# Background operations of ScalarE and VectorE ordered behind the newest weight split of their engine, and the gate logarithms' exponential taken ahead of the copies

## The chip, the core and the metric

The kernel runs on one core of one Trainium2 chip. The metric is the device time of one execution in microseconds (us). The core has five engines with instruction queues of their own: TensorE (PE, matrix products), ScalarE (ACT, element functions and copies), VectorE (DVE, two-operand arithmetic), GpSimd (POOL) and SyncE (SP, which here only issues DMAs). Each engine works through its queue in the order of the program; engines wait for each other by semaphores. PE reads its operands from the on-chip memory (SBUF) and adds into accumulators (PSUM).

## The reference

A trunk of two layers over 256 positions of width 2048. Each layer normalises its input, multiplies it by one wide matrix `w_in`, runs eight mLSTM heads (matrix memory, part A) and eight RG-LRU blocks (gated linear recurrence, part B) side by side, multiplies both results by `w_out` and adds them to the input. A last normalisation follows. Everything is float32.

```python
def hybrid_layer(x, ...):
    u = rms_norm(x, norm_g)
    qk, v, o, z_a, ig, fg, xb, z_b = jnp.split(u @ w_in, SPLIT_AT, axis=-1)
    q, k = jnp.split(jax.nn.silu(causal_dwconv(qk, qk_conv)), 2, axis=-1)
    i_pre = ig + i_bias
    log_f = jax.nn.log_sigmoid(fg + f_bias)
    h = mlstm_chunkwise(q, k * DK_A ** -0.5, v, i_pre, log_f)
    h = h * jax.nn.sigmoid(o)
    h = ((h - mu) * lax.rsqrt(var + EPS)) * head_norm_g      # per head
    y_a = h * jax.nn.silu(z_a)
    xc = causal_dwconv(xb, lru_conv_w) + lru_conv_b
    y_b = rg_lru(xc, w_a, b_a, w_x, b_x, lam) * jax.nn.silu(z_b)
    return x + jnp.concatenate([y_a, y_b], axis=-1) @ w_out

def rg_lru(x, w_a, b_a, w_x, b_x, lam):
    r, i = sigmoid(x @ w_a + b_a), sigmoid(x @ w_x + b_x)    # in blocks of 256
    a = jnp.exp(-8.0 * r * softplus(-lam))
    u = x * i * jnp.sqrt(1 - a * a)
    return scan(h_t = a_t * h_{t-1} + u_t)
```

The mLSTM's result at time t needs exponentials of differences of the gates' running sums: `exp(F_t - F_s + i_s - m_t)` for s up to t. The kernel takes all 256 positions as one chunk.

## The kernel before

**Products.** A float32 product is made of three products in a shorter float format: each operand is split into a high part H and a rest L, and H·H, H·L and L·H are added. The weights come from DRAM in 268 tiles of 128 x 2048 (`raw`), each of them two halves, called units here and numbered 1 to 536 in the order of the program. `prepare` splits a unit: ScalarE copies it rounded (`wH`, line 308), VectorE subtracts (`wL`, `tt_`, lines 167–168). Twelve matmuls on PE (`mm_a`, line 332) use the unit; the second of them is the first that needs `wL`. The pool `wsp` holds four units' H and L, so `wH` of unit k must wait until PE is done with unit k-4, and the splits run at most three units ahead of PE.

**Everything else** (normalisation, convolutions, gates, recurrences, the heads' small products, the layout changes through DRAM that `swapped` makes) runs on ScalarE, VectorE and GpSimd between the splits. These background operations are written as Python generators in the list `bg`. After each unit's matmuls the main loop (lines 1099–1114) calls `pump`, which lets the generators issue operations until a budget of estimated us is spent; a generator that yields "wait" is passed over. The order in which `pump` issues is only the order of writing: a scheduler of the framework then fixes the order of each engine's queue, and places an operation whose inputs are ready earlier ahead of splits that were written before it. `order(a, b)` adds a dependence without a semaphore: a stands behind b in the queue, nothing else.

**The places that matter below.** For each layer l there are four head groups g of two heads.

- `rms_stats`, `rms_bcast`: the layer's normalisation factor `rstd` (sum, square root with a table load on ScalarE, reciprocal on VectorE); it is laid along the diagonal in `dg`, which PE multiplies with ones (`ps_rb`) and VectorE copies to `rb`. `o_post` uses `rstd` in the sigmoid `so`, which empties the accumulator of the layer's first chunk.
- `gates_gen`, `gates_tr`: the heads' input and forget gates as 8 rows; their running sums leave for DRAM (`nG_d`, line 538), their transposed values `sb` are copied by GpSimd into 128 rows (`at`, line 554, eight copies), and one half of the copies is exponentiated (`em`, line 555).
- `e_gen`: `nb` (line 564, GpSimd's DMA queue) reads `nG_d` back on all rows; VectorE adds, ScalarE exponentiates `E` (line 576), GpSimd clears the upper triangle (`affine_select`, line 579). There is one `nb` and one `E`.
- `qk_post`, `xb_post`, `zb_post`: a chunk of `u @ w_in` is scaled by ScalarE (`tok`), transposed by VectorE, moved by four SP DMAs (`moved`) and fetched back by a DMA of GpSimd's queue (`fr`, line 450). ScalarE then copies it (`ch`, line 470), and the convolution (`qc`, `xc`) follows.
- `gate_half`, `gate_post`: the RG-LRU gates. Sigmoids, exponentials and tanh on ScalarE, then on VectorE `gate1·xc`, `Dt`, `a`, `Dt`, `a`, `gate1·Dt`, `gate1·gate0` and four scans `xc` (line 795); `zb_post` makes `zb`, `ybH` and `ybL` of them, `z_post` makes `yaH` and `yaL`; these four are PE's operands in the products with `w_out`.

ScalarE's functions live in tables; where the next function isn't in the loaded table, an ACT_TABLE_LOAD stands ahead of it.

## Time and profile before

| | |
|---|---|
| time, median of 3 runs | 1495.64 us (1495.3 to 1496.07) |
| the profiled execution's own time | 1495.12 us |
| its span in the trace | 1493.4 us |
| mean granted TensorE clock | 0.999 |
| VectorE / ScalarE / GpSimd busy | 1049.7 / 915.3 / 75.5 us |
| DMA | 345.66 MB, 231 GB/s mean |

The span is what the trace covers from the first to the last instruction; the execution's own time is 1.7 us longer, for what lies around it. A row of a timeline reads: start, duration, engine, line, operation, out<-in, shape, and in brackets how long the engine had been idle before and what ended it; "x2" joins two instructions of a kind that follow each other. Matmuls overlap: each is drawn 0.39 us long, while the next starts 0.23 us after it.

### The profile page before, as it was taken

What the parts mean: (1) busy time and instruction counts of PE and PEld (TensorE: products, weight loads), DVE (VectorE), ACT (ScalarE), POOL (GpSimd) and SP (SyncE); (2) the same over time, 40 slices, a digit from 0 to 9 for tenths busy, and PEclk for the clock granted to TensorE, in tenths of its full rate; (3) what the DMA queues carried; (4) which work ended last, traced back from release to release, by engine and by line L of the source; (5) the groups of instructions that cost most, each with busy time, mean ns of one, the idle gap of its engine ahead of it and who ended that gap; (6) DMA issues with size and microseconds to landing.
All of it is one profiled execution on the core that took longest, in us unless ns stands there. A gap on an engine that the chain in (4) does not pass through costs nothing.

```text
span 1493.4 us, 18544 instructions
## 1 busy us (share of the span) xinstructions
PE 1482.0 (99%) x6894; PEld 1240.3 (83%) x6894; DVE 1049.7 (70%) x1406; ACT 915.3 (61%) x1160; POOL 75.5 (5%) x154
## 2 busy tenths in 40 slices
PE   9999999999999999999999999999999999999997
PEld 7888888888888888888888888888888888888886
DVE  6778976675567855678867697766855778556785
ACT  6656754575456854558675577645754567555675
POOL 0010000000000000000000200000000000000002
PEclk9999999999999999999999999999999999999999
DMA  9866667866577666876786667568666776578783
GB/s 329 303 224 220 222 224 210 253 225 215 200 239 233 216 224 218 259 255 226 264 287 195 227 211 247 196 210 251 222 227 210 226 239 227 205 229 265 232 282 112
DMA packets 91370, 345.66 MB, mean 231 GB/s; under 512 B 9984, under 2 KB 30480, under 8 KB 69776
## 3 DMA queue, kind: packets, MB, share of 16 engines
q1 hardware_dynamic: 79472, 306.44, 60.2%
q0 software_dynamic: 9344, 33.58, 9.1%
q10 hardware_dynamic: 2464, 4.47, 0.8%
q8 instruction: 54, 0.88, 0.2%
q14 instruction: 36, 0.29, 0.1%
HBM read 307.20 MB, written 37.24 MB: 231 GB/s over the span
## 4 chain that ended last, share of the span: by engine, by line
PE 94%; DVE 2%; ACT 1%; DMA 1%; issue 1%; POOL 0%; SPq 0%; ACTq 0%; DVEq 0%; POOLq 0%
PE acc L332 84%; PE ps_gt L751 3%; PE acc L345 1%; DVE wL L168 1%; PE acc L993 1%; PE acc L992 1%; PE acc L994 1%; DMA fr<-moved 1%; PE acc_x L993 0%; PE acc_x L992 0%; PE acc_x L994 0%; DMA raw<-in_ws_dram 0%; ACT wH L308 0%; PE ps_n L587 0%; PE ps_n L585 0%
## 5 line engine op out<-in xcount | busy, mean ns | idle before, releaser
L332 PE MATMUL acc<-wH,x_s 128*128 128x512 f32 x3008 | 930.4, 389 | 0.9 <-ACT wH L308 0.9
L168 DVE TENSOR_TENSOR wL<-raw,wH 128x1024 fp32r<-128x1024 f32 (+1 forms) x532 | 636.2, 1203 | 352.0 <-ACT wH L308 351.8
L308 ACT CAST wH<-raw 128x1024 fp32r<-128x1024 f32 (+1 forms) x532 | 547.0, 1037 | 393.2 <-PE acc L332 353.6
L332 PEld LDWEIGHTS acc<-wH,x_s 128*128 128x128 f32 x3008 | 564.5, 188 | 118.6 <-ACT wH L308 1.8
L332 PE MATMUL acc<-wL,x_s 128*128 128x512 f32 x1504 | 584.2, 389 | 0.9 <-DVE wL L168 0.8
L332 PEld LDWEIGHTS acc<-wL,x_s 128*128 128x128 f32 x1504 | 282.3, 188 | 59.6 <-DVE wL L168 1.6
L332 PE MATMUL acc<-wH,yaH 128*128 128x512 f32 x224 | 87.4, 390 | 0.0
L332 PE MATMUL acc<-wH,ybL 128*128 128x512 f32 x224 | 87.3, 390 | 0.0
L332 PE MATMUL acc<-wH,yaL 128*128 128x512 f32 x224 | 87.2, 389 | 0.0
L332 PE MATMUL acc<-wL,ybH 128*128 128x512 f32 x224 | 87.2, 389 | 0.0
L332 PE MATMUL acc<-wH,ybH 128*128 128x512 f32 x224 | 87.2, 389 | 0.0
L332 PE MATMUL acc<-wL,yaH 128*128 128x512 f32 x224 | 87.2, 389 | 0.0
L450 POOL DMA_DIRECT2D fr<-moved x34 | 18.8, 552 | 729.3 <-DMA moved<-blk 561.6
L332 PEld LDWEIGHTS acc<-wH,ybL 128*128 128x128 f32 x224 | 42.0, 188 | 9.0 <-DVE ybL L168 0.3
L332 PEld LDWEIGHTS acc<-wH,yaL 128*128 128x128 f32 x224 | 42.1, 188 | 9.0
L332 PEld LDWEIGHTS acc<-wH,ybH 128*128 128x128 f32 x224 | 42.1, 188 | 8.5
L332 PEld LDWEIGHTS acc<-wL,ybH 128*128 128x128 f32 x224 | 42.1, 188 | 8.5
L332 PEld LDWEIGHTS acc<-wL,yaH 128*128 128x128 f32 x224 | 42.1, 188 | 8.3
L332 PEld LDWEIGHTS acc<-wH,yaH 128*128 128x128 f32 x224 | 42.1, 188 | 8.2
L446 DVE STREAM_TRANSPOSE blk<-tok 128x1024 f32<-128x1024 f32 x33 | 40.8, 1237 | 11.0 <-ACT tok L436 11.0
L436 ACT ACTIVATE tok<-acc,rstd 128x512 f32<-128x512 f32 x46 | 29.1, 685 | 31.1 <-PE acc L332 31.0
L890 ACT COPY stage<-acc 128x1024 f32<-128x1024 f32 x24 | 24.4, 1015 | 34.4 <-PE acc L332 34.2
(209 smaller groups left out, 1291.9 us busy)
## 6 DMA issues: line engine op xcount, KB each, us to landing
raw<-in_ws_dram SPq DMA_DIRECT2D x168, 1024.0 KB, 5.2
raw<-in_ws_dram SPq DMA_DIRECT2D x190, 512.0 KB, 5.1
fr<-moved POOLq DMA_DIRECT2D x34, 512.0 KB, 6.9
moved<-blk SPq DMA_DIRECT2D x132, 128.0 KB, 2.6
x_d<-stage POOLq DMA_DIRECT2D x24, 512.0 KB, 5.5
x_d<-x_acc ACTq DMA_DIRECT2D x8, 512.0 KB, 8.4
x_acc<-x_d SPq DMA_DIRECT2D x8, 512.0 KB, 4.2
xp<-in_xt_dram SPq DMA_DIRECT2D x8, 256.0 KB, 7.2
```

The lines of the kernel that those rows point to most:

```text
L168: return V.tensor_tensor(out=o, in0=a, in1=b, op=op)
L308: st["wH"] = S.copy(out=H[:, o], in_=r[:, o])
L332: st["mm"] = PE.matmul(o, a_[:, kt, P * t : P * t + P], W[:, k], start=b, stop=z)
L345: PE.matmul(ps[:, ct, T * part : 2 * T], W[:, k, P * ct : P * ct + P], moving, start=first and k == 0 and part == 0, stop=last and k == 3 ...
L436: S.activation(out=by_block(tok, t), in_=acc[:, t, :].rearrange("p (c m j) -> p c m j", c=4, m=4), func=AF.Copy, scale=rstd[:, t : t + 1])
L446: V.transpose(out=blk.rearrange("p m n -> p (m n)"), in_=tok.rearrange("p m c t j -> p (m c t j)"))
L450: back.dma_start(out=fr.rearrange("p a c t i -> p a (c t i)"), in_=moved)
L751: PE.matmul(o, W[:, ib, jl], xs[:, ib, a, :], start=j == 0 and i == 0 and W is Hv and a == 0, stop=i == 1 and W is Lv, skip_group_check=True)
L890: S.copy(out=stage, in_=ps)
L992: PE.matmul(o, yH[:, kt, tsl], Hv[:, k, cs], start=start and k == 0, stop=False)
L993: PE.matmul(o, yH[:, kt, tsl], Lv[:, k, cs], start=False, stop=False)
L994: PE.matmul(o, yL[:, kt, tsl], Hv[:, k, cs], start=False, stop=stop and k == 1)
```

## The change

The change has three parts. First, the handles of VectorE and ScalarE are wrapped (`Behind`): while `pump` runs, from the ninth unit on (`st["tie"]`), every operation that it issues on VectorE is ordered behind the newest `wL`, and every one on ScalarE behind the newest `wH`. As `prepare` has run three units ahead by then, the newest split belongs to the unit three later than the one whose matmuls have just been issued; the scheduler can no longer put the operation ahead of that split. Second, in `gates_tr` the fixed number of waits is replaced by one for the first `nb`; the exponential is taken on `sb[32:64]` in place (32 x 256) ahead of GpSimd's copies, and the copies are ordered behind the `nb` DMA. Third, the exponential of `E` and the square root of `sd` are ordered behind the newest `wH`.

```diff
+    class Behind:
+        def __init__(self, eng, key):
+            self.eng, self.key = eng, key
+        def __getattr__(self, name):
+            op = getattr(self.eng, name)
+            if name == "dma_start":
+                return op
+            def f(*a, **k):
+                ins = op(*a, **k)
+                if st.get("tie"):
+                    order(ins, st[self.key])
+                return ins
+            return f
+    V, S = Behind(V, "wL"), Behind(S, "wH")
...
     def gates_tr(l):
         yield None
         yield None
-        for _ in range(2 + 2 * l):
+        while ("nb", l, 0) not in st:
             yield "wait"
+        sb = st["sb"]
+        order(S.activation(out=sb[32:64], in_=sb[32:64], func=AF.Exp), st["wH"])
...
-                G.tensor_copy(out=at[q_][32 * a : 32 * a + 32], in_=sv[32 * q_ : 32 * q_ + 32, :, a, 0:NH])
-        S.activation(out=em, in_=em, func=AF.Exp)
+                cp = G.tensor_copy(out=at[q_][32 * a : 32 * a + 32], in_=sv[32 * q_ : 32 * q_ + 32, :, a, 0:NH])
+                order(cp, st["nb", l, 0])
...
-        nc.gpsimd.dma_start(out=nb.rearrange("p h t -> p (h t)"), in_=src)
+        st["nb", l, g] = nc.gpsimd.dma_start(out=nb.rearrange("p h t -> p (h t)"), in_=src)
...
-        S.activation(out=E, in_=E, func=AF.Exp)
+        order(S.activation(out=E, in_=E, func=AF.Exp), st["wH"])
...
-            S.activation(out=sd, in_=mv[:, :, :, 1], func=AF.Sqrt, bias=epst)
+            order(S.activation(out=sd, in_=mv[:, :, :, 1], func=AF.Sqrt, bias=epst), st["wH"])
...
+        st["tie"] = n >= 8
         pump(1.05 if len(bg) <= 2 else 2.6)
+        st["tie"] = False
```

In the changed program nearly every operation of ScalarE and VectorE bears the wrapper's line, 101; and ScalarE has 62 table loads where it had 56. The rest of the instructions are the same, in other places; PE's order is the same but for four rows at the boundary of the layers.

**VectorE, first layer, first group, units 62 to 67** (the RG-LRU gates, with `yaL` of part A; gate_1450 is `gate1`, gate_1415 is `gate0`; "x2" stands for two of a kind). Before:

```order
175 L171 SCALAR_TENSOR_TENSOR a<-gate_1415,Dt 128x1024
176 L168 TENSOR_TENSOR wL<-raw,wH 128x1024 x2
177 L171 SCALAR_TENSOR_TENSOR Dt<-a,Dt 128x1024
178 L176 TENSOR_SCALAR a<-Dt 128x1024
179 L171 SCALAR_TENSOR_TENSOR gate_1450<-gate_1450,Dt 128x1024
180 L168 TENSOR_TENSOR wL<-raw,wH 128x1024
181 L168 TENSOR_TENSOR gate_1450<-gate_1450,gate_1415 128x1024
182 L168 TENSOR_TENSOR wL<-raw,wH 128x1024
183 L795 SCALAR_TENSOR_TENSOR xc<-a,gate_1450 128x256 x3
184 L168 TENSOR_TENSOR wL<-raw,wH 128x1024
185 L795 SCALAR_TENSOR_TENSOR xc<-a,gate_1450 128x256
186 L168 TENSOR_TENSOR wL<-raw,wH 128x1024
```

and with the change:

```order
171 L101 TENSOR_TENSOR wL<-raw,wH 128x1024
172 L101 SCALAR_TENSOR_TENSOR a<-gate_1415,Dt 128x1024
173 L101 TENSOR_TENSOR wL<-raw,wH 128x1024
174 L101 SCALAR_TENSOR_TENSOR Dt<-a,Dt 128x1024
175 L101 TENSOR_TENSOR wL<-raw,wH 128x1024
176 L101 TENSOR_SCALAR a<-Dt 128x1024
177 L101 SCALAR_TENSOR_TENSOR gate_1450<-gate_1450,Dt 128x1024
178 L101 TENSOR_TENSOR wL<-raw,wH 128x1024
179 L101 TENSOR_TENSOR gate_1450<-gate_1450,gate_1415 128x1024
180 L101 TENSOR_TENSOR yaL<-tok,yaH 128x1024
181 L101 SCALAR_TENSOR_TENSOR xc<-a,gate_1450 128x256 x4
182 L101 TENSOR_TENSOR wL<-raw,wH 128x1024
```

Row 176 of before holds the `wL` of units 62 and 63; row 171 of the change is that of unit 63, row 186 and row 182 are that of unit 67. Three gate operations (`gate1·xc`, the first `Dt`, and `a`) stood ahead of unit 62's split; now the first two stand between the splits of units 62 and 63, and `a` behind that of 63. `gate1·gate0` and the scans lay between three splits, and `yaL` behind unit 67's; now `gate1·gate0`, `yaL` and all four scans stand together ahead of unit 67's. The second layer has the same rows, at units 326 to 331.

**ScalarE, start of the second layer, units 288 to 292** (`rstd` and `so`; `gwp` are the gates' weights). Before:

```order
363 L383 ACT_TABLE_LOAD
364 L383 ACTIVATE rstd<-ms,epst 128x2
365 L308 CAST wH<-raw 128x1024 x2
366 L463 ACTIVATE tok<-fr,pars 128x256 x4
367 L308 CAST wH<-raw 128x1024
368 L465 CAST x_s<-tok 128x4x256
369 L308 CAST wH<-raw 128x1024 x6
370 L596 ACT_TABLE_LOAD
371 L596 ACTIVATE so<-acc,rstd 128x512 x2
372 L308 CAST wH<-raw 128x1024 x2
373 L436 ACTIVATE tok<-acc,rstd 128x4x4x32 x2
```

and with the change:

```order
384 L101 CAST x_s<-tok 128x4x256
385 L101 CAST wH<-raw 128x1024 x6
386 L101 CAST gwp<-gwr_105 128x8x8 x4
387 L101 CAST wH<-raw 128x1024
388 L101 ACT_TABLE_LOAD
389 L101 ACTIVATE rstd<-ms,epst 128x2
390 L101 CAST wH<-raw 128x1024
391 L101 ACT_TABLE_LOAD
392 L101 ACTIVATE so<-acc,rstd 128x512 x2
393 L101 ACTIVATE tok<-acc,rstd 128x4x4x32 x2
```

The square root of `rstd` with its table load stood nine splits ahead of `so`; now only one split, unit 291's, lies between them, and a second table load.

**GpSimd, first layer, second group** (the fetch `fr` of the q and k chunk is row 28 in both). Before:

```order
24 L564 DMA nb<-nG_d_117 128x512
25 L579 AFFINE_SELECT E<-E 128x128 x4
26 L450 DMA fr<-moved 128x1024
27 L604 MEMSET vH 128x4x2
28 L450 DMA fr<-moved 128x1024
```

and with the change:

```order
24 L470 DMA fr<-moved 128x1024 x2
25 L626 MEMSET vH 128x4x2
26 L586 DMA nb<-nG_d_117 128x512
27 L601 AFFINE_SELECT E<-E 128x128 x4
28 L470 DMA fr<-moved 128x1024
```

The group's `affine_select`, which waits for the exponential of `E` on ScalarE, and the next `nb`, which waits for VectorE's reads of the old one, have moved from well ahead of that `fr` to directly ahead of it. On ScalarE the exponential of this `E` now stands behind the split of unit 73, and the copy `ch` that waits for the `fr` behind that of unit 75, as before.

## The prediction

> **What bounds the kernel now.** I read the busy shares first, then the chain that ended last, then what PE waits for.

> ```profile
> PE 1482.0 (99%) x6894; PEld 1240.3 (83%) x6894; DVE 1049.7 (70%) x1406; ACT 915.3 (61%) x1160; POOL 75.5 (5%) x154
> PE 94%; DVE 2%; ACT 1%; DMA 1%; issue 1%; POOL 0%; SPq 0%; ACTq 0%; DVEq 0%; POOLq 0%
> L308 ACT CAST wH<-raw 128x1024 fp32r<-128x1024 f32 (+1 forms) x532 | 547.0, 1037 | 393.2 <-PE acc L332 353.6
> ```

> PE is busy 99% of the span, and the chain is PE for 94%. The third row says who waits for whom: ScalarE stood idle 353.6 us ahead of `wH` until PE released a buffer. The splits are ready early, so an operation on ScalarE or VectorE costs nothing until it makes a split late. The question is only where PE stands still, before and after.

> ```profile
> PE acc L332 <- ACT wH L308: 0.9, 1, 0.9
> PE acc L332 <- DVE wL L168: 0.8, 1, 0.8
> 839.40 0.74 PE L332 MATMUL acc<-wH,x_s 128*128 128x512 f32 x2
> 840.94 0.50 PE L332 MATMUL acc<-wL,x_s 128*128 128x512 f32 x1 [0.80 <-DVE wL L168]
> 898.81 0.61 PE L332 MATMUL acc<-wH,x_s 128*128 128x512 f32 x2
> 899.48 0.50 PE L332 MATMUL acc<-wL,x_s 128*128 128x512 f32 x1
> ```

> In the waits of PE just two stand against the splits. The second is that at 840.94: after two matmuls from 839.40, one each 0.23, it was due at 839.87 and came 1.07 late. A smaller one hides at 899.48, due at 899.27: 0.21. A matmul behind a stall is drawn 0.50 instead of 0.39, and its follower comes 0.11 later still. So the two stalls together hold 1.07 + 0.21 + 0.22 = **1.5 us**. That is all that the change can take out: 0.1%.

> **The part on the gates takes it out.**

> ```profile
> 828.17 4.72 POOL L554 COPY at<-scs 32x16 f32<-32x16 f32 x8
> 832.84 0.56 POOL L564 DMA_DIRECT2D nb<-nG_d  x1
> 832.92 0.21 ACT L555 ACTIVATE at<-at 128x16 f32<-128x16 f32 x1 [5.64 <-POOL at L554]
> ```

> ScalarE stood 5.64 us for GpSimd's eight copies, with splits queued behind; that made unit 306 late at 840.94. With the exponential ahead of the copies this goes. `nb` may now leave about 4.7 us earlier and the copies follow, so VectorE's use of both comes at much the same time; behind it `wL` of units 304 to 309 stay tight. Between nothing and a second stall of about half the old one I take **+0.3** (0 to 0.6). The stall at 899.48 goes because `a` no longer stands ahead of unit 326's split. Credit **-1.5**.

> **The RG-LRU gates behind the splits, twice.** In before these VectorE operations filled the wait for unit 326's `wH`; tied, they cannot.

> ```profile
> 157.10 1.04 ACT L308 CAST wH<-raw 128x1024 fp32r<-128x1024 f32 x1
> 896.94 1.99 ACT L308 CAST wH<-raw 128x1024 fp32r<-128x1024 f32 x2
> 895.46 0.69 DVE L176 TENSOR_SCALAR Dt<-Dt 128x1024 f32<-128x1024 f32 x1 [1.00 <-ACT Dt L768]
> 897.06 1.23 DVE L171 SCALAR_TENSOR_TENSOR a<-gate,Dt 128x1024 f32<-128x1024 f32 x1 [0.91 <-ACT gate L774]
> 898.21 2.35 DVE L168 TENSOR_TENSOR wL<-raw,wH 128x1024 fp32r<-128x1024 f32 x2
> ...
> 910.36 1.20 DVE L168 TENSOR_TENSOR wL<-raw,wH 128x1024 fp32r<-128x1024 f32 x1
> 911.48 1.22 DVE L168 TENSOR_TENSOR yaL<-tok,yaH 128x1024 fp32r<-128x1024 f32 x1
> 173.54 0.39 PE L332 MATMUL acc<-wL,x_s 128*128 128x512 f32 x1
> 913.22 0.39 PE L332 MATMUL acc<-wL,x_s 128*128 128x512 f32 x1
> ```

> Rows by engine: the `wH` of units 62 and 326, VectorE from 895.46, and the matmuls that need `wL` of units 67 and 331. From the start of unit 326's `wL` (898.21) to that of unit 331's (910.36) VectorE ran without a gap for 12.15. The new order puts four more operations into that stretch: `gate1·xc` and `yaL`, 1.14 each (1.22 less an overlap of 0.08 with what follows), `a`, 1.15 (897.06 to 898.21), and `Dt`, 0.61 (0.69 less the overlap). That is 16.2; with the split's 1.20, 17.4; less about 0.1 for a dependent pair that is no longer adjacent, 17.3. The stretch can start when `wH` is done: at 157.10 + 1.04 + 0.05 = 158.19 in the first layer, 898.03 in the second. So unit 67's `wL` ends at 175.5, and its matmul stood at 173.54: **+1.9**. Unit 331's ends at 915.3; its matmul, 0.32 earlier without the old stall, at 912.9: **+2.4**. Nothing else hides this: the cover was VectorE's idle time ahead of units 62 and 326. After the stall the splits of units 68 to 70 have 0.2 to 0.5 us left by the same count.

> **GpSimd's queue, twice.** `fr` of the second group now stands behind `nb` and `affine_select`, hence behind ScalarE's exponential of `E`.

> ```profile
> 183.19 0.53 POOL L450 DMA_DIRECT2D fr<-moved  x1 [12.32 <-ACT wH L308]
> L579 POOL TENSOR_SCALAR_AFFINE_SELECT E<-E x32: 282/284/659, 88.9 to 1193.6; 128x128 f32<-128x128 f32 x32
> L576 ACT ACTIVATE E<-E x8: 846/847/852, 87.9 to 1191.9; 128x768 f32<-128x768 f32 x8
> 181.68 1.06 ACT L308 CAST wH<-raw 128x1024 fp32r<-128x1024 f32 x1 [1.61 <-PE acc L332]
> 192.12 1.05 ACT L470 COPY ch<-fr 128x1024 f32<-128x1024 f32 x1 [3.94 <-DMA fr<-moved]
> 195.29 2.44 DVE L171 SCALAR_TENSOR_TENSOR qc<-ch,pars,qc 128x255 f32<-128x255 f32 x6
> 198.02 0.39 PE L332 MATMUL acc<-wL,x_s 128*128 128x512 f32 x1
> 200.74 0.39 PE L332 MATMUL acc<-wL,x_s 128*128 128x512 f32 x1
> ```

> All times here keep step with PE. The split of unit 73 ends at 182.74; a table load (1.28), `E` (0.85) and four selections (0.66 and three of 0.28) follow: about 186.4, so `fr` is issued 3.2 us later than at 183.19. If it again takes 8.9 us, `ch` starts near 195.4 and `wH` of unit 76 stands behind it: done at 197.5, its `wL` at 198.7, needed at 198.02: 0.7 to 0.9. Six convolution operations (2.44) lie ahead of unit 77's `wL`: 202.4, needed at 200.74 plus what is lost already: another 0.9. So at most 1.8; nothing if `fr` lands in its median of 6.9 us (the table of DMA issues). I take **+1.2**. The second layer has the same rows with `fr` at 922.81 landing in 8.4: at most 0.9, **+0.5**. In the third and fourth groups the splits behind `ch` are over 4 us early: nothing.

> **The start of the second layer.**

> ```profile
> 781.34 1.05 ACT L308 CAST wH<-raw 128x1024 fp32r<-128x1024 f32 x1 [1.67 <-PE acc L332]
> 782.41 1.28 ACT L596 ACT_TABLE_LOAD   x1
> 784.06 1.27 ACT L596 ACTIVATE so<-acc,rstd 128x512 f32<-128x512 f32 x2 [0.37 <-PE acc L332]
> 789.07 0.62 PE L332 MATMUL acc<-wH,x_s 128*128 128x512 f32 x2
> ```

> `so` empties the accumulator that unit 289's first matmul takes at 789.30 (the second of the last row). Now `rstd` is behind unit 290's `wH`, which PE releases one unit (2.72) after 781.34: 784.06 to 785.11; table and square root to 786.7; unit 291's `wH`, released at 786.78, to 787.83; table to 789.1; `so` to 790.4. **+1.1**.

> **Two smaller places.**

> ```profile
> 47.47 0.48 DVE L175 TENSOR_SCALAR dg<-ident,rstd 128x128 fp32r<-128x128 f32 x2
> 48.40 1.22 DVE L168 TENSOR_TENSOR wL<-raw,wH 128x1024 fp32r<-128x1024 f32 x1
> 49.60 0.40 PE L400 MATMUL ps_rb<-dg,ones 128*128 128x256 f32 x2
> 713.47 0.69 DVE L168 TENSOR_TENSOR zb<-zsg,xc 128x512 f32<-128x512 f32 x1
> 714.28 1.22 DVE L168 TENSOR_TENSOR wL<-raw,wH 128x1024 fp32r<-128x1024 f32 x1
> 715.66 0.39 PE L332 MATMUL acc<-wH,ybH 128*128 128x512 f32 x1
> ```

> At 47.47 four `dg` operations (0.93 to 48.40) trade places with unit 24's split. They end at about 50.4, and the second `ps_rb` matmul stood at 49.7: **+0.6**. At the boundary `zb` (0.69) comes behind unit 264's split (to 715.5) and `ybH` behind that, about 716.8, needed at 715.66: 1.1 late, unless PE's four moved rows cover it. Between 0 and 1.1 I take **+0.5**.

> **Sum.** -1.5 + 0.3 + 1.9 + 2.4 + 1.2 + 0.5 + 1.1 + 0.6 + 0.5 = 7.0, and 0.11 for each of some five restarts: **+7.5 us**. From the profiled execution's own 1495.12 that gives **1502.6**; the median, 1495.64, is 0.5 above that execution, which is inside the runs' spread. With every open cost at its lower end the sum is 4.9 (1500.0), at its upper end 9.5 (1504.6).

> The six added table loads (6 x 1.28 = 7.7 us) cost nothing by themselves, ScalarE being 61% busy, except in the chains above, where they are counted. [...] The trace bears out the load alone: at 782.41 the load begins 0.02 after the split and the engine is free at 783.69.

> **The rivals.**

> - *The bursts don't reach PE* (15%). The place is `wH` of units 62 and 326: if ScalarE reaches them 1.9 and 2.4 us sooner, VectorE's stretch starts sooner and both stalls vanish, and with them 4.3 + 0.2. For it: by PE alone these `wH` could run earlier; they stand behind exponentials and tanh. Against it: those eight operations and their table load keep their place. With the open costs at their lower ends this gives 1495.12 + 4.9 - 4.5 = 1495.5, not slower.
> - *Only the sure terms at about half* (13%): the bursts alone, all else covered: 1495.12 - 1.5 + 4.3 + 0.2 = 1498.1, at the border of what can be told.
> - *Only the credit* (3%): every tie hidden: 1493.6.
> - *More than counted* (14%). GpSimd's queue is strict, so every group's `fr`, not only the second's, may come late, or ScalarE's blocks pass on from one split to the next. Where a delay spreads over one more unit it costs its size again, 0.9 to 1.8 at four places: about 1507. [...]
> - *The forecast*, 1499 to 1505: 55%.

> A measurement of this kernel can tell about 0.2% (3 us) from no change. The range of 1496.5 to 1506.5 leaves out the rival of the credit, half of the first and a part of the fourth. Faster by over 0.2%, below 1492.6, needs more than all stalls that there are: 1%, out of the third rival. Within 0.2%: the rest of the first three rivals, 30%. Slower: the forecast and the fourth rival, 69%.

> **What would show it.** In the profile after: PE waiting for `wL` near 173 and 915, about 2 us each; for `so` near 790; near 198 behind `ch`; no wait near 840 and none of ScalarE for `at`. I am wrong if VectorE is idle ahead of units 67 and 331, or if `fr` of the second group is issued less than 2 us later against PE than before.

## The result, and the profile after

| | before | changed |
|---|---|---|
| time, median | 1495.64 us (1494.96 to 1496.07, 5 runs) | 1504.77 us (1502.46 to 1506.11, 5 runs) |
| ratio, 95% interval | 1 | 1.0062 (1.0052 to 1.0073) |
| profiled execution's own time / span | 1495.12 / 1493.4 us | 1505.44 / 1503.7 us |

The change costs 9.1 us, 0.6%. The forecast was 1502.6, in a range of 1496.5 to 1506.5.

From the page of the changed kernel, the busy line and the group of `wH`:

```profile
PE 1486.5 (99%) x6894; PEld 1241.5 (83%) x6894; DVE 1062.6 (71%) x1406; ACT 924.2 (61%) x1166; POOL 72.8 (5%) x154
L101 ACT CAST wH<-raw 128x1024 fp32r<-128x1024 f32 (+1 forms) x532 | 547.9, 1037 | 410.0 <-PE acc L352 369.0
```

Nothing stands out here: the engines do the same work, and ScalarE waits for PE even longer than before. (The page's chain, PE 94% before, reads PE 44% here only because it could be followed back no further than the wait for `so` at 797.) The loss is in places, and the waits of PE in the changed kernel show them (sum, times, longest):

```profile
PE acc L352 <- DVE wL L101: 5.6, 6, 1.8
PE ps_blank L130 <- DVE blank L101: 1.3, 1, 1.3
PE acc L352 <- ACT so L101: 1.0, 1, 1.0
PE acc L352 <- ACT ybH L101: 0.3, 1, 0.3
PE ps_rb L420 <- DVE dg L101: 0.3, 1, 0.3
PE acc L352 <- ACT wH L101: 0.2, 1, 0.2
```

Here a wait counts only from the drawn end of the last matmul, so each place loses more than its row says. Counted from start to start over PE's matmuls, with what follows at once (a matmul behind a stall starts 0.11 later than it should), the places are:

| near (us) | what came late | forecast | lost |
|---|---|---|---|
| 49 | `dg` for `ps_rb` | 0.6 | 0.9 |
| 174 | unit 67's `wL`, behind the RG-LRU operations | 1.9 | 2.0 |
| 177 | half-speed matmuls behind that stall | 0 | 1.6 |
| 204 | a split behind `fr` and `ch` | 1.2 | 0.7 |
| 717 | `ybH`, `ybL` at the layers' boundary | 0.5 | 0.6 net |
| 760 | a split behind the boundary's work on ScalarE | 0 | 1.5 |
| 796 | `so` | 1.1 | 1.3 |
| 840 to 850 | second stall behind the gates | 0.3 | 0 |
| 919 | unit 331's `wL` | 2.4 | 2.0 |
| 946, 950 | splits behind the second layer's `fr` | 0.5 | 1.5 |
| 840, 899 of before | gone | -1.5 | -1.5 |

Together with 0.2 near 107 that is 10.8; the opening of this execution was 0.7 shorter, so 10.1 of the span's 10.3. The forecast's 0.5 for restarts is inside the right column. PE's rows at four of the places:

```profile
205.30 0.50 PE L352 MATMUL acc<-wL,x_s 128*128 128x512 f32 x1 [0.39 <-DVE wL L101]
760.95 0.50 PE L352 MATMUL acc<-wL,x_s 128*128 128x512 f32 x1 [0.76 <-DVE wL L101]
797.45 0.50 PE L352 MATMUL acc<-wH,x_s 128*128 128x512 f32 x1 [1.05 <-ACT so L101]
921.84 0.50 PE L352 MATMUL acc<-wL,x_s 128*128 128x512 f32 x1 [1.76 <-DVE wL L101]
```

VectorE's rows from 158 on in the changed kernel (start, duration, instruction), and PE's two that matter near 174:

```profile
158.49 1.22 DVE L101 TENSOR_TENSOR wL<-raw,wH 128x1024 fp32r<-128x1024 f32 x1 [5.01 <-ACT wH L101]
...
168.79 1.22 DVE L101 TENSOR_TENSOR wL<-raw,wH 128x1024 fp32r<-128x1024 f32 x1
169.92 1.21 DVE L101 TENSOR_TENSOR gate<-gate,gate 128x1024 f32<-128x1024 f32 x1
171.06 1.22 DVE L101 TENSOR_TENSOR yaL<-tok,yaH 128x1024 fp32r<-128x1024 f32 x1
172.19 2.43 DVE L101 TENSOR_TENSOR_SCAN xc<-a,gate 128x256 f32<-128x256 f32 x4
174.54 1.20 DVE L101 TENSOR_TENSOR wL<-raw,wH 128x1024 fp32r<-128x1024 f32 x1
```

```profile
173.41 0.61 PE L352 MATMUL acc<-wH,x_s 128*128 128x512 f32 x2
175.79 0.50 PE L352 MATMUL acc<-wL,x_s 128*128 128x512 f32 x1 [1.77 <-DVE wL L101]
```

VectorE stood idle 5.01 us ahead of unit 62's split, in which before it had done three of these operations, and then worked without a gap until unit 67's `wL` was done at 175.74. From the first `wL` to the last it took 16.05 us; PE's matmul stood at 175.79.

And what no step of the forecast had: PE's granted clock in four stretches of the changed kernel (busy time and count of PE, PEld, DVE, ACT and POOL; the last three columns are the clock as a share of full speed, the DMA share and GB/s):

```profile
170.00:173.60 3.60, 3.60 (x17) 3.00 (x16) 3.60 (x6) 3.59 (x4) 0.00 (x0) 1.00 0.66 234
173.60:176.50 2.90, 1.13 (x5) 0.62 (x5) 2.90 (x4) 2.63 (x4) 0.11 (x1) 1.00 0.17 71
176.50:180.40 3.90, 3.90 (x12) 3.03 (x11) 3.90 (x5) 0.47 (x1) 0.00 (x0) 0.56 0.29 76
180.40:190.00 9.60, 9.60 (x43) 7.92 (x43) 7.92 (x12) 6.80 (x8) 1.57 (x6) 1.00 0.87 280
```

### The profile page after: what moved, and what is told of

Read it like the earlier page. It is cut to its first block, busy times and chain, and to the rows that moved or that the text cites. A ratio compares the mean times of both kernels' runs of the same rounds, so it can differ in the third digit from the quotient of the medians.

```text
span 1503.7 us, 18545 instructions
## 1 busy us (share of the span) xinstructions
PE 1486.5 (99%) x6894; PEld 1241.5 (83%) x6894; DVE 1062.6 (71%) x1406; ACT 924.2 (61%) x1166; POOL 72.8 (5%) x154
## 5 line engine op out<-in xcount | busy, mean ns | idle before, releaser
L101 ACT CAST wH<-raw 128x1024 fp32r<-128x1024 f32 (+1 forms) x532 | 547.9, 1037 | 410.0 <-PE acc L352 369.0
L101 DVE SCALAR_TENSOR_TENSOR qc<-ch,pars,qc 128x255 f32<-128x255 f32 (+2 forms) x96 | 44.7, 480 | 9.6 <-ACT qc L101 8.1
L101 DVE SCALAR_TENSOR_TENSOR xc<-ch,pars,xc 128x255 f32<-128x255 f32 (+2 forms) x96 | 43.6, 479 | 6.0 <-ACT xc L101 4.7
```

The lines of the kernel that those rows point to most:

```text
L101: ins = op(*a, **k)
```

## The experiments

All but the two probes were timed against the kernel before; the ratio stands with its 95% interval. Each builds on the changed kernel unless said otherwise; "untied" means that a generator's operations are issued with `st["tie"]` off.

| run | median us | ratio to before |
|---|---|---|
| e1, no ties | 1493.60 | 0.9988 (0.9978 to 0.9998) |
| e2, tie on ScalarE alone | 1496.11 | 1.0008 (0.9998 to 1.0017) |
| e3, tie on VectorE alone | 1509.52 | 1.0092 (1.0077 to 1.0107) |
| e4, RG-LRU gates untied | 1497.36 | 1.0014 (1.0005 to 1.0024) |
| e5, `e_gen` untied | 1505.60 | 1.0068 (1.0053 to 1.0083) |
| e6, first chunk untied | 1504.00 | 1.0057 (1.0040 to 1.0074) |
| e7, only the RG-LRU gates tied | 1500.73 | 1.0038 (1.0025 to 1.0051) |
| e10, three generators untied | 1499.07 | 1.0025 (1.0016 to 1.0035) |
| e11, ties without the part on the gates | 1504.76 | 1.0064 (1.0047 to 1.0080) |
| e12, four generators untied | 1494.53 | 0.9997 (0.9987 to 1.0007) |

### e1: the change without the ties

```diff
-        st["tie"] = n >= 8
+        st["tie"] = False
```

> The change without the ties of the background operations (the wrapper passes everything through; the gates' exponential ahead of the copies, the nb DMA first, and the order of E and sd stay). My theory: only the two old stalls of PE (1.07 + 0.11 near 840, perhaps the 0.3 near 899) go and nothing new comes: 0.3 to 1.5 us under before, 1494 to 1495.4, with no PE wait near 174, 204, 796, 919 or 946. Rival (the part on the gates costs time itself, because nb and the copies now stand in a row on GpSimd): over 1497, with a new wait of PE for a split near 80 to 90 or 830 to 850.

Measured: 1493.60, 1.7 us under before. PE's waits:

```profile
PE ps_blank L130 <- DVE blank L101: 1.3, 1, 1.3
PE acc L352 <- ACT wH L101: 1.0, 1, 1.0
```

Both rows lie in the opening. After that PE's matmuls follow each other to the end, but for 0.11 us near 717. So the part on the gates (with the orders of `E` and `sd`, which e1 keeps) is worth its credit without the ties, and the whole loss of 11.2 us (1504.77 - 1493.60) is the ties'. This version is faster than both kernels, though by only 0.1% against the one before.

### e2 and e3: the tie on one engine

```diff
-    V, S = Behind(V, "wL"), Behind(S, "wH")
+    S = Behind(S, "wH")          # e2
...
+    V = Behind(V, "wL")          # e3
```

> The change with the tie on ScalarE alone. My theory: the waits of PE belong to single places. The two bursts on VectorE (2.0 us each near 174 and 919, and the half-clock stretch of 1.6 us behind the first) and the wait for dg near 49 (0.8) go; what hangs on ScalarE's tie stays: 0.6 near 204, 1.3 near 796, up to 1.5 near 946. Sum against before: +2 to +4 us, 1497.5 to 1499.5. Rival (the loss is spread: each tie shortens the run-ahead of the splits everywhere): about half of the 9 us, many small waits, no single place over 1.5. Rival (the six added table loads): they are ScalarE's, so nearly all of the 9 us stays.

> The change with the tie on VectorE alone. My theory: the bursts near 174 and 919 stay with 2.0 us each, with a half-clock stretch of 1.6 us behind one of them in some executions, and dg near 49 with 0.8; rstd at the start of the second layer is free on ScalarE but its sum waits on VectorE, so the wait for so near 796 shrinks to under 1; the fetches near 204 and 946 stay behind VectorE's writing of E and lose 0 to 1. Sum against before +4 to +8 us: 1500 to 1503.5. Rival (spread): about half of the 9 us without the two single waits of 2 us. Rival (table loads): about as fast as before, since its table loads are few.

Measured: e2 1496.11, under its expected range, and e3 1509.52, over it. In e2 the bursts are gone as expected, but the waits near 204, 796 and 946, which I had put down to ScalarE's tie, are gone too; three others, of 1.4, 0.5 and 0.7 us near 49, 89 and 109, are there. The waits near 204, 796 and 946 therefore need VectorE's tie. The one near 796 needs nothing else: e3 has it whole (1.3), with ScalarE free. Its rows, of the changed kernel, e3 and e2 in turn:

```profile
791.05 0.15 DVE L101 TENSOR_REDUCE ms<-ss 128x2 f32<-128x8 f32 x1
793.37 0.30 ACT L101 ACTIVATE rstd<-ms,epst 128x2 f32<-128x2 f32 x1
...
790.32 0.16 DVE L101 TENSOR_REDUCE ms<-ss 128x2 f32<-128x8 f32 x1
792.64 0.30 ACT L403 ACTIVATE rstd<-ms,epst 128x2 f32<-128x2 f32 x1
...
786.69 0.29 ACT L101 ACTIVATE rstd<-ms,epst 128x2 f32<-128x2 f32 x1
```

The square root `rstd` waits for the sum `ms` on VectorE. The tie holds `ms` back to 791.05, from 751.9 before; in e2 it runs at 754.3, and the root 2.2 us earlier against PE than in the changed kernel.

e3 loses more than both ties together. Besides the bursts, PE waits near 853, 885 and 908. ScalarE's rows of e3 ahead of the second of these:

```profile
884.09 0.62 ACT L753 CAST xcs<-xc 128x512 fp32r<-128x512 f32 x1 [1.89 <-DVE xc L101]
884.62 1.99 ACT L328 CAST wH<-raw 128x1024 fp32r<-128x1024 f32 x2
```

The free engine still has its operations far ahead, but their inputs now come late from the tied one. ScalarE waits 1.89 us for `xc` with two splits queued behind; ahead of the other two places it waits 2.43 us for `qc` and 3.02 for `mv`. Neither rival holds: the loss lies in single places, and both kernels have 62 table loads, as the changed one has; e1, the fastest of all, has 63.

### e4 and e7: the RG-LRU gates untied, and tied alone

```diff
-        bg.append(gen())              # at the end of gate_post
+        bg.append(untied(gen()))      # e4: all else tied
...
+        bg.append(tied(gen()))        # e7: all else free
```

> The change with the operations of the RG-LRU gates (the generator of gate_post, on both engines) left untied, all else tied. My theory: the two bursts vanish, and with them 2 x 2.0 us and the half-clock stretch of about 1.6 us in those executions that have it: 4 to 6 us under the changed kernel, 1498.5 to 1501; the spread of the times falls to that of before (about 1 us); the waits near 49, 204, 760, 796 and 946 stay. Rival (the burst only shows where a general lack of lead becomes visible): the wait comes back a few units later with about the same size, and the time stays over 1502.

> The reverse: only gate_post's generator tied, on both engines, all other operations as free as before the change (the part on the gates stays). My theory: the two bursts near 174 and 919 are whole, about 2 us of PE each, the wait near 760 too (it went when this generator alone was untied), a half-clock stretch of 1.6 us in some executions, nothing near 49, 204, 796 and 946: 1493.6 + 4 to 7 = 1497.6 to 1500.6, with a wider spread than 1 us. Rival (a burst needs the other ties to become late): under 1496.

Measured: e4 1497.36, 7.4 us under the changed kernel and 1.1 below its expected range; e7 1500.73, 7.1 us over e1. In e4 the waits near 174, 919, 717 and also 760 are gone; near 49 (2.2), 204 (0.3), 791 (1.3) and 940 (1.1) they stay. e7 has just the reverse: both bursts with 2.0 each, 0.6 at the boundary, 1.8 near 757. The two halves add up: 7.1 for this generator alone and 3.8 for all others (1497.36 - 1493.60) make 10.9 of the 11.2. One generator, with eleven operations on VectorE in each group, makes about two thirds of the loss, and needs no other tie for it. e4's spread did not fall to 1 us (1495.23 to 1499.76); why is not shown.

### e5 and e6: E untied, the first chunk untied

```diff
-        bg.append(e_gen(l, g))
+        bg.append(untied(e_gen(l, g)))                # e5, and E's order behind wH taken out
...
-            chunk_in(l, kind, g, lambda a: bg.append(first_gen(a)), layer_start(l))
+            chunk_in(l, kind, g, lambda a: bg.append(untied(first_gen(a))), layer_start(l))   # e6
```

> The change with only e_gen untied (the writing of E on VectorE and its exponential on ScalarE, as far ahead as before). My theory: GpSimd's affine_select and nb stand well ahead of the second group's fr again, so fr leaves about 3 us earlier against PE and the waits near 204 (0.65) and 946 (1.45) go; the bursts near 174 and 919 and the places near 49, 760 and 796 stay: about 2 us under the changed kernel, 1501.5 to 1504. Rival (those waits come from ScalarE's table load and the shifted convolution, not from fr): fr's issue moves, but the waits stay and the time is as the changed kernel's.

> The change with only the first chunk's generator untied (rstd, its diagonal dg, the gates' rows, their copies). My theory: dg and rstd stand ahead again, and the waits near 49 (0.8) and 796 (1.3) go; the one near 760 (1.5) goes only if the gates' preparation at the layer's start makes it: 2 to 3.6 us under the changed kernel, 1500 to 1503. Rival: with rstd early the wait near 796 is taken over by the sigmoid's other inputs and stays over 1.

GpSimd's rows in the changed kernel, and ScalarE's copy that waited:

```profile
186.31 0.54 POOL L586 DMA_DIRECT2D nb<-nG_d  x1 [11.44 <-DVE E L101]
188.98 1.03 POOL L601 TENSOR_SCALAR_AFFINE_SELECT E<-E 128x128 f32<-128x128 f32 x4 [2.12 <-ACT E L101]
189.96 0.55 POOL L470 DMA_DIRECT2D fr<-moved  x1
198.49 1.05 ACT L101 COPY ch<-fr 128x1024 f32<-128x1024 f32 x1 [6.26 <-DMA fr<-moved]
```

`fr` left only when `nb` had waited for VectorE's reads of the old one and `affine_select` for ScalarE's exponential. In e5 it left at 186.55, which is 2.2 us earlier against PE's matmuls, and the waits near 204 and 946 are gone. The time did not follow: 1505.60, no better than the changed kernel and above the expected range. In its place e5 has 2.4 us near 904, which e10 and e12 explain, and a burst near 919 that grew to 2.1. e6 lost the waits near 49 and 796 as expected and found 1.5 near 104 to 108, where `wL` waits behind the first group's work on q and k: 1504.00, too little. Its profiled execution has half-speed matmuls behind both bursts, where the changed kernel's has them behind one.

e6 also lost the waits near 204 and 946, which I had not expected, and it shows their second condition:

```profile
191.11 0.55 POOL L481 DMA_DIRECT2D fr<-moved  x1
197.90 1.05 ACT L101 COPY ch<-fr 128x1024 f32<-128x1024 f32 x1 [4.53 <-DMA fr<-moved]
```

Against PE `fr` left as late as in the changed kernel (2.8 us later than in the kernel before), but it landed after 6.8 us instead of 8.5, and PE did not wait; e11, with 6.8, has no wait near 204 either. In e5 it took 8.6 us but left early. So in these runs PE waits near 204 only when `fr` both leaves late and lands slowly.

The wait near 760 stayed in e6, so it isn't the gates' preparation; with e4 and e7 it belongs to the RG-LRU tie. In its place in the changed kernel ScalarE waited 2.48 us for an `fr` of the boundary, with the next split and the sums of squares behind it; by which step the tie delays that `fr` I did not follow.

### e8 and e9: the clock by itself

Both are the kernel before with a hold ahead of twelve `wL`; e9 makes it shorter. Each was executed once.

```diff
+    def hold(r, prev):
+        two, one = HOLDS[st["unit"]]
+        for i in range(two + one):
+            ins = tt_(r, r, r, ALU.max) if i < two else ts_(r, r, 1.0, ALU.mult)
+            order(ins, prev)
+            prev = ins
+        return prev
...
+            last = hold(r, st["wL"]) if st["unit"] in HOLDS else None
             st["wL"] = tt_(L[:, o], r[:, o], H.bitcast(F32)[:, o], ALU.subtract)
+            if last is not None:
+                order(st["wL"], last)
```

> The kernel before with VectorE held up ahead of twelve units' wL by seven to nine extra passes over the raw weights (maximum of a value with itself, or times one: values unchanged), so that PE stands still for 1 to 4 us at twelve places far apart. It measures the clock by itself. [...]

> As the probe before (the kernel before with VectorE held up ahead of twelve units' wL, values unchanged), with fewer passes: PE should stand still for 1 to 3 us at twelve places. The first probe's stalls, 3.6 to 7 us, were all followed by half-speed matmuls; stalls of 1.3 us and less in all kernels so far by none; of those of 1.9 to 2.1 us some were and some not. [...] Theory B (a fixed threshold of the idle time itself): all stalls above one length, none below it.

Measured: e8's stalls came out longer than meant, 3.6 to 7.0 us, and each of the twelve was followed by half-speed matmuls. e9's lie at 2.88 and below. Two of its stalls are equal to 0.01 us; PE's rows of both, first the one from 469.51, then the one from 1412.57:

```profile
471.85 0.50 PE L347 MATMUL acc<-wL,ybH 128*128 128x512 f32 x1 [1.96 <-DVE wL L168]
...
472.71 0.63 PE L347 MATMUL acc<-wL,ybH 128*128 128x512 f32 x1
473.14 0.63 PE L347 MATMUL acc<-wH,ybL 128*128 128x512 f32 x1
...
1414.92 0.50 PE L347 MATMUL acc<-wL,ybH 128*128 128x512 f32 x1 [1.96 <-DVE wL L168]
...
1415.73 0.40 PE L347 MATMUL acc<-wL,ybH 128*128 128x512 f32 x1
1415.97 0.40 PE L347 MATMUL acc<-wH,ybL 128*128 128x512 f32 x1
```

The first pair starts 0.43 apart, the second 0.24. PE's granted clock during and after both stalls (columns as above):

```profile
469.50:472.00 2.50, 0.54 (x3) 0.15 (x2) 2.50 (x7) 1.03 (x1) 0.00 (x0) 1.00 0.00 0
472.00:476.00 4.00, 4.00 (x11) 3.14 (x12) 4.00 (x7) 0.00 (x0) 0.00 (x0) 0.57 0.75 272
1412.50:1415.00 2.50, 0.54 (x4) 0.12 (x2) 2.50 (x7) 1.05 (x1) 0.00 (x0) 1.00 0.00 0
1415.00:1419.00 4.00, 4.00 (x18) 3.27 (x19) 4.00 (x7) 1.22 (x2) 0.00 (x0) 1.00 0.80 252
```

PE was busy for 0.54 us in both stretches with the stall; the mean clock of the next 4 us is 0.57 behind the first and 1.00 behind the second. Over the profiled executions of all kernels here, the two probes included, the opening left out:

| lost by the stall, us | stalls | followed by half speed |
|---|---|---|
| 0.5 to 1.9 | 46 | 0 |
| 1.92 to 1.93 | 10 | 3 |
| 2.12 to 2.13 | 4 | 3 |
| 2.35 and 2.88 | 2 | 2 |
| 3.57 to 7.03 | 12 | 12 |

The changed kernel has such a pair too, both of 1.92 to 1.93: behind the stall near 174 the clock is 0.50 from 176.96 to 180.37, 3.41 us long, and from 920 to 930, through and behind the one near 919, it is 1.00. Equal stalls with and without half speed behind them speak against a fixed threshold of the idle time (B). The ties aren't needed for it, since the probes have none. What decides between two equal stalls is not shown.

### e11: the ties without the part on the gates

```diff
-        while ("nb", l, 0) not in st:
+        for _ in range(2 + 2 * l):
             yield "wait"
...
+        S.activation(out=em, in_=em, func=AF.Exp)
```

> The change without its part on the gates (gates_tr as before: the fixed number of waits, GpSimd's copies ahead of nb, the small exponential behind the copies), all ties kept. My theory: the parts add up; the part on the gates was worth 1.7 us alone, so its absence costs 1 to 2.5 us: 1505.5 to 1507.5, with a wait of PE near 845 to 850. Rival (the ties alone remove that stall, since the exponential can no longer stand ahead of a split that is ready): no wait there, 1504 to 1505.5.

Measured: 1504.76, the same as with it, and no wait of PE near 845: the rival holds. With the ties the stall of before is gone either way, so the part on the gates and the ties earn the same 1.5 us, once.

### e10 and e12: three and four generators untied

e10 takes e4, e5 and e6 together; e12 also unties the heads' generator in `qk_post`, which makes `sd`.

> The change with three generators untied: gate_post, e_gen and the first chunk's; everything else tied. My theory: with the three largest sources gone, no stall over 1 us is left; what remains are places of some tenths where the untied stand ahead of the tied (as near 105 with only the first chunk's untied): 1494 to 1496.5, at or a little over the kernel without any ties (1493.6). Rival (the other ties cost as much once these are gone): over 1497.

> As with the three generators untied, and the heads' generator (qk_post's, which makes the mean and variance mv and the square root sd) untied as well. In the run before, ScalarE loaded three tables between two splits near 886 because the tied sd came between the two sigmoids sz, and PE stood 2.4 us near 899 behind it. My theory: those loads cause it; with sd ahead again the stall near 899 goes (to at most the 0.3 of the kernel before) and the time falls by 2.4 us, or by some 4 where the clock had followed it: 1494.5 to 1497. Rival (the RG-LRU gates' exponentials alone hold unit 326's split back, loads or not): a stall over 1 us stays near 899, and the time stays over 1497.5.

Measured: e10 1499.07, where I expected at most 1496.5; e12 1494.53. ScalarE in e10, between two splits of the second layer, and PE behind it:

```profile
883.55 1.28 ACT L101 ACT_TABLE_LOAD   x1
885.15 0.69 ACT L101 ACTIVATE sz<-acc,rstd 128x512 f32<-128x512 f32 x1 [0.32 <-PE acc L363]
885.86 1.28 ACT L101 ACT_TABLE_LOAD   x1
887.16 0.30 ACT L101 ACTIVATE sd<-mv,epst 128x4 f32<-128x4 f32 x1
887.47 1.28 ACT L101 ACT_TABLE_LOAD   x1
888.77 0.69 ACT L101 ACTIVATE sz<-acc,rstd 128x512 f32<-128x512 f32 x1
```

```profile
899.88 0.51 PE L363 MATMUL acc<-wH,x_s 128*128 128x512 f32 x1 [0.98 <-ACT wH L101]
901.34 0.50 PE L363 MATMUL acc<-wL,x_s 128*128 128x512 f32 x1 [0.95 <-DVE wL L101]
```

The tied square root came between the two sigmoids `sz`: three table loads, 3.8 us, where the kernel before needed two. PE lost 2.4 us 11 us later, at unit 326, which has no lead there; e5 has the same rows. With the heads untied ScalarE is back at 56 table loads, the stall shrinks to 0.7 (0.3 was expected), and the time falls by 4.5, to the lower end of what was expected. The theory holds over its rival, but the stall near 899 is only 1.7 of the fall: waits of 0.9 near 105 to 108 and 0.7 near 912 went with it, and since the whole generator was untied, the loads are not tested apart from its other operations. What is still tied in e12 costs 0.9 us over e1 and gains nothing.

## Why the prediction was right

- **What bounds it, and the credit (-1.5).** Right: PE's stalls and the half-speed stretch behind one of them are the whole story, and e1 shows the credit without the ties (-1.7). The forecast added it to the ties; e11 shows that the ties take out the same stall by themselves. The sum holds only because it was counted once. The 0.3 near 899 needed no tie: in e1 `a` still stands ahead of unit 326's split, and the stall is gone.
- **The RG-LRU gates, 1.9 and 2.4.** Right in mechanism and place, 2.0 each in size. Unit 331's was mis-sized by 0.4: I had moved PE's need 0.3 earlier and kept ScalarE where it was, while unit 326's `wH` also came earlier against PE; the stretch began 15.4 us ahead of the need, not 14.9. What I left out is that this tie also costs 1.5 near 760 and the half-clock stretch; e7 makes it 7.1 of the 11.2.
- **GpSimd's queue, 1.2 and 0.5.** The mechanism is shown by e5 and e6 together: against PE `fr` left 2.8 us later than before (forecast 3.2) in the changed kernel and in e6, and 0.5 later in e5; and as the forecast said, a landing near the median (6.8 in e6) costs nothing. The sizes were 0.7 and 1.5, by the landing: in the first layer `ch` began 8.5 us after the issue of `fr`, less than the 8.9 that I took for the upper end; in the second `fr` left 3.6 late and took 8.6, over the 8.4 that I took, and two splits came late, not one.
- **The start of the second layer, 1.1.** Right, 1.3: `so` began at 796.13 behind two table loads, by the steps of the forecast. e6 removes it. What the forecast did not name is the tie that puts `rstd` there: it is VectorE's, on the sum `ms` (e2 and e3).
- **The smaller places, 0.6 and 0.5.** 0.9 and 0.6. **The second stall near 840, 0.3:** did not come.
- **Table loads as free except in the chains.** So in the changed kernel; but e10 shows one place where two more of them cost PE 2.4 us. In e10 the switch cost the load of 1.28 us and hardly more: `sd` starts 1.32 us after the sigmoid ends.
- **The clock.** The sum has no price for half-speed matmuls; here 3 of 10 stalls of 1.92 to 1.93 us had them behind, for 1.6 us each. Half clock is in the trace of before too: 0.50 in its last 3.2 us (from 1490.17), with PE at rest. Without the stretch the profiled execution would have been at 1503.8, and the fastest of the five runs (1502.46, with the highest granted clock, 0.999) lies at the forecast; the median is two us above. Whether the unprofiled runs differ by such stretches is not shown: one takes only 0.001 off the mean clock (half of 3.41 in 1503.7 us), the last digit on record.

The forecast's size thus came out right partly by compensation, which is luck: 0.5 too much each near 204 and for restarts, 0.4 near 919 and 0.3 at 840 to 850, against 1.0 too little near 946 and the 1.5 near 760 and 1.6 of clock that it did not have. Its mechanisms for the bursts, for `fr` and for `so` are borne out; the step behind the 1.5 near 760 stays open.

## What to carry to other kernels

Where one engine is busy 99%, find the few places where the others have no lead and price an ordering rule there alone: "behind the newest split" costs nothing in most of this kernel, 0.6 to 1.5 us at six places, and 2 us at two, because there it took away the idle time in which long chains used to run. A rule on one of two coupled engines can be worse than on both, since the free engine's operations then stand ahead of urgent work and wait for late inputs. Undo a rule generator by generator before throwing it away or keeping it: here the small part, the gates' exponential ahead of the copies, is worth 1.7 us without the ties, and nothing with them.

## What the hardware showed unexpectedly

A stall of PE of 1.92 to 1.93 us was followed by 7 to 8 matmuls at half speed (0.43 us each; near 174 in the changed kernel the granted clock was 0.50 for 3.41 us) in 3 of 10 cases, one of 2.12 to 2.13 in 3 of 4, and none of the 46 shorter than 1.9; each such stretch cost 1.6 to 1.7 us, nearly the price of the stall again. So two equal stalls of one execution differed in what they cost: in the changed kernel 2.0 us near 919, and 2.0 + 1.6 near 174. What decides it is not shown. How much of the spread of the times comes from this is not shown: the changed kernel's five runs lie 3.7 us apart and those of before 1.1, but the four of e11, with the same two bursts, 0.7.
